# Keys and values of an attention block from float32r parts in three passes, and a sum of squares moved to GpSimd

## The chip, the cores and the metric

One core of a Trainium2 chip runs the whole program as a single launch. The metric is device time in microseconds (us), the median of several executions. Below, PE is the matmul engine (TensorE) and PEld its weight loads, DVE is VectorE, ACT is ScalarE, POOL is GpSimd, and SP is the queue engine that issues most transfers.

## The reference

A block of a hybrid model over 512 tokens and 16 meta tokens (T = 528 rows), all in float32. What matters here is the latent attention: queries, keys and values of 16 heads come from two small normalised latents, `cq` (384 wide) and `ckv` (256 wide).

```python
n1 = _rmsnorm(h, norm1_g[l])
xr, gr, cq, ckv, kr, g_rnn, g_att = jnp.split(n1 @ w_in[l], IN_SPLITS, axis=-1)
hr = _rg_lru(_causal_conv(xr, ...), ...)
y_rnn = (hr * jax.nn.gelu(gr)) @ w_rnn_out[l]
q = (_rmsnorm(cq, q_norm_g[l]) @ w_uq[l]).reshape(B, Tp, 16, 64 + 32)
kv = (_rmsnorm(ckv, kv_norm_g[l]) @ w_ukv[l]).reshape(B, Tp, 16, 64 + 64)
o = _mla_attention(q_nope, q_rope, kv[..., :64], k_rope, kv[..., 64:])
y_att = o @ w_attn_out[l]
mixed = jax.nn.sigmoid(g_rnn) * y_rnn + jax.nn.sigmoid(g_att) * y_att
h = h + mixed @ w_out[l]
h = h + _peer(_rmsnorm(h, norm2_g[l]), ...)    # 8 heads choose 16 of 16384 experts per token
```

## The kernel before

Everything is laid out with features on the 128 partitions. Most products are taken in three passes of float32r matmuls (`mm3`): each operand is split into a high part, cast by ACT, and a low part, subtracted by DVE (`split`), and high x high, high x low and low x high are added in PSUM. A few small products are plain float32 matmuls; the profile shows each of these as two records.

The stages follow one another:

- From 0 to about 48 us: norms, and the latents. `sq` holds their squares; `bcast_rms` multiplies them by a matrix of ones (float32) to sum over partitions and spread the sum, once for each 128-wide part: two parts for `ckv` (`kvn`), three for `cq` (`qn`).
- To about 184 us: the recurrent branch (`xr_tile`, `gates`, `gr_tile`, `gate_att`). `latent_norms` (line 300) is traced inside its first step, after `xr_tile(1)`: reciprocals of the two norms (`rk`, `rq`), and the latent `kvf` scaled to its final value.
- To about 472 us: attention, interleaved with the output of the recurrent branch (`out_rnn`) and the last `gate_att` tiles, which serve as work for PE between the steps of the attention. The heads go in eight pairs. `att_pair(pr)` makes the keys and values of a pair and asks for the query weights `wa`; it is called in the middle of the pair before, `att_query` later in it.
- Then the mixing, the choice of experts, and from about 960 us the dense and gathered expert products, to the end.

The order on each engine is made at compile time by a list scheduler: of the instructions that are ready it takes the one written first. Three shared resources matter in the attention:

- `wload` streams weights through a ring: three raw tiles (`RB`) and three split tiles (`WB`) of 512 columns (five in the stage before). `wa` takes two of the three split tiles from its cast to the last query product, `wgn` and `wrnn` of `out_rnn` two each. The weights of keys and values have a private tile, `wkv`, in plain float32, outside the ring.
- All products that `att_pair` and `att_query` make go through one PSUM tile, tag `am` (`rings`, line 446): the next product starts when ACT and DVE have taken the last one out.
- `vms`, `vfh`, `vfl` hold the values of two pairs in turn.

Of the kernel before, what the change touches and what calls it, by code (L numbers as in the profile page):

```python
# [8 lines left out]
F32 = mybir.dt.float32  # L9
F32R = mybir.dt.float32r  # L10
# [9 lines left out]
P = 128  # L20
D = 1024
NK = 8
NM = 16
S = 512
# [40 lines left out]
def r32(t):  # L65
    return t.bitcast(F32)
# [52 lines left out]
def hybrid_block_kernel(ctx: ExitStack, tc, hT, x, win, wkr, vecs, wgate, wrnn, watt, wuq, wukv, wout,  # L119
# [4 lines left out]
    def pool(stack, name, side="left", **kw):  # L124
        return stack.enter_context(tc.tile_pool(name=name, bufs=1, side=side, reuse_waits="tile", **kw))
# [21 lines left out]
    onesP = cp.tile([P, P], F32, name="onesP")  # L147
    one_t = cp.tile([P, 1], F32, name="one_t")
    eps_t = cp.tile([P, 1], F32, name="eps_t")
    efx = [cp.tile([P, NS], F32, name=f"efx{c}") for c in range(4)]  # L150
    gate = [cp.tile([P, NS], F32, name=f"gate{c}") for c in range(4)]
    ky = cp.tile([P, 2, P], F32, name="ky")

    def split(dst_hi, dst_lo, src):
        A.copy(dst_hi, src)  # L155
        V.tensor_sub(dst_lo, src, r32(dst_hi))  # L156
# [28 lines left out]

    cqh = fa.tile([P, 3, S], F32R, name="cqh")
    cql = fa.tile([P, 3, S], F32R, name="cql")
    kvf = fa.tile([P, 2, T], F32, name="kvf")
    tabq = fa.tile([P, S], F32, name="tabq")

    kth = [fa.tile([P, T], F32R, name=f"kth{i}") for i in range(NKB)]
# [11 lines left out]
    def bcast_rms(sq, pieces, dim, dst, name):  # L203

        for t0, n in pieces:
            o = mm1(f"{name}_ss{t0}")
            for k, q in enumerate(sq):
                TE.matmul(o[:, :n], onesP, q[:, t0:t0 + n], start=k == 0, stop=k == len(sq) - 1)
            A.activation(dst[:, t0:t0 + n], o[:, :n], AF.Sqrt, bias=eps_t, scale=1.0 / dim)
# [58 lines left out]
    krt = rg_tile("gr", "krt")  # L268
    tk, ka, kr = krt[0:64, 0, :], krt[64:96, 1, :], krt[64:96, 2, :]
    mk = rp.tile([P, P], F32, name="mk")  # L270
    nc.sync.dma_start(tk, cst[0:64, 768:768 + T])
    nc.sync.dma_start(ident, cst[:, 0:128])
    nc.sync.dma_start(mk, cst[:, 128:256])
    nc.sync.dma_start(tabq, cst[:, 256:768])
    nc.sync.dma_start(iota, cst[:, 1312:1440])
    nc.sync.dma_start(cand_f, cst[:, 1888:1888 + NCAND])
    nc.sync.dma_start(ky, keysT.rearrange("p (a n) -> p a n", a=2))
    V.tensor_mul(tk, tk, rb[0:64, :])
    sq = two(("rr", "ii"), "sq2")
    for k in range(2):  # L280
        for t0, n, o in lat[k]:
            V.tensor_mul(kvf[:, k, t0:t0 + n], o[:, :n], rb[:, t0:t0 + n])
        A.activation(sq[k], kvf[:, k, :], AF.Square)
    for k in range(3):
        (t0, n, o), = now(proj_tile(k, False, f"wcq{k}"))
        cq = hp.tile([P, S], F32, tag="sg", bufs=2, name=f"cq{k}")
        gk = vec[:, V_QG + k:V_QG + k + 1]
        V.tensor_mul(cq, o, rb[:, NM:])
        A.activation(sq[2 + k][:, :S], cq, AF.Square)
        A.activation(cqh[:, k, :], cq, AF.Identity, scale=gk)  # L290
        V.scalar_tensor_tensor(cql[:, k, :], cq, gk, r32(cqh)[:, k, :], op0=OP.mult, op1=OP.subtract)
    for t0, n, o in now(proj_tile(None, True, "wkr", wkr, 64)):
# [1 line left out]
        V.tensor_mul(kr[:, t0:t0 + n], o[32:64, :n], tk[32:64, t0:t0 + n])  # L294
    rk = rp.tile([P, T], F32, name="rk")
    rq = rp.tile([P, S], F32, name="rq")
    bcast_rms(sq[0:2], TT, 256, rk, "kvn")
    bcast_rms(sq[2:5], ((0, S),), 384, rq, "qn")

    def latent_norms():  # L300

        V.tensor_add(kr, kr, ka)
        split(kth[0][64:96, :], ktl[0][64:96, :], kr)
        for i in range(NKB):
            for r0 in (64, 96):
                if (i, r0) != (0, 64):
                    nc.gpsimd.dma_start(kth[i][r0:r0 + 32, :], kth[0][64:96, :])
                    nc.gpsimd.dma_start(ktl[i][r0:r0 + 32, :], ktl[0][64:96, :])
        V.reciprocal(rk, rk)
        for k in range(2):  # L310
            V.scalar_tensor_tensor(kvf[:, k, :], kvf[:, k, :], vec[:, V_KVG + k:V_KVG + k + 1], rk,
                                   op0=OP.mult, op1=OP.mult)
        V.reciprocal(rq, rq)
        V.tensor_mul(tabq, tabq, rq)
        V.tensor_copy(ident_b, ident)
        V.tensor_copy(mask_b, mk)
# [139 lines left out]
    def mma(name):  # L456
        return ps_ring("att", name)
# [9 lines left out]


    MK = 64 + NM
    vms = [ap.tile([P, P], F32R, name=f"vm{i}") for i in range(2)]  # L470
    pms = [ap.tile([P, 2 * P], F32R, name="pm")]
    zero = ap.tile([P, T], F32, tag="p", bufs=PB, name="zero")
    V.memset(zero, 0.0)
    for t in vms + pms:
        V.tensor_copy(t, zero[:, :t.shape[-1]])

    def att_pair(pr):

        wkv = ap.tile([P, 2, 2, P], F32, tag="wkv", bufs=1, name=f"wkv{pr}")
        nc.sync.dma_start(wkv, wukv[pr].rearrange("p (a k m) -> p a k m", a=2, k=2))  # L480
        vh = ap.tile([P, 4, P], F32R, tag="vfh", bufs=2, name=f"vfh{pr}")
        vl = ap.tile([P, 4, P], F32R, tag="vfl", bufs=2, name=f"vfl{pr}")
        vm = vms[pr % 2]
        for t0, n in TT:
            o = mma(f"k{pr}_{t0}")
            for k in range(2):
                TE.matmul(o[:, :n], wkv[:, 0, k, :], kvf[:, k, t0:t0 + n], start=k == 0, stop=k == 1)
            if t0:
                for k in range(2):
                    TE.matmul(o[:NM, 384:512], kvf[:, k, 0:NM], wkv[:, 1, k, :], start=k == 0, stop=k == 1)  # L490
                A.copy(vm[0:NM, :], o[:NM, 384:512])
                A.copy(vm[32:32 + NM, :], o[:NM, 384:512])
                V.tensor_sub(vm[64:64 + NM, :], o[:NM, 384:512], r32(vm)[0:NM, :])
            for j in range(2):
                b = (2 * pr + j) % NKB
                A.copy(kth[b][0:64, t0:t0 + n], o[64 * j:64 * j + 64, :n])
                V.tensor_sub(ktl[b][0:64, t0:t0 + n], o[64 * j:64 * j + 64, :n], r32(kth[b])[0:64, t0:t0 + n])

        o = mma(f"v{pr}")
        for c in range(4):  # L500
            t0 = NM + c * P
            for k in range(2):
                TE.matmul(o[:, c * P:(c + 1) * P], kvf[:, k, t0:t0 + P], wkv[:, 1, k, :], start=k == 0, stop=k == 1)
        split(vh, vl, o.rearrange("p (c m) -> p c m", m=P))
        pair = dict(v=(vh, vl, vm), w=wload(wuq[pr], 768, f"wa{pr}"), q=[])
        return pair

    def att_query(pr, j, pair):

# [205 lines left out]
    ctx.enter_context(dx)  # L715
    actp = pool(dx, "act", "right")
    vp = pool(dx, "vstream", "right")
    po_ = pool(postx, "choice")
    scx = ExitStack()
    sp_ = pool(scx, "scat", "right")  # L720
    tv = [po_.tile([P, PH, 2, TOPK], F32, name=f"tv{i}") for i in range(4)]
# [317 lines left out]
def _layout(i):  # L1039
    f = {k: np.asarray(v) for k, v in i.items()}  # L1040
    x = f["x"].reshape(S, D)
    h = np.concatenate([f["meta_tokens"], x], 0)
    a = {}
    a["hT"] = h.T.reshape(NK, P, T).transpose(1, 0, 2).reshape(P, NK * T)
    a["x"] = x

    def tiles(w):
        kk, n = w.shape
        return w.reshape(kk // P, P, n // P, P).transpose(2, 1, 0, 3).reshape(n // P, P, kk)

    w = f["w_in"][0]
    o = np.cumsum([0, 1024, 1024, 384, 256, 32, 1024, 1024])
    xr, gr, cq, ckv, kr, grn, gat = (w[:, o[j]:o[j + 1]] for j in range(7))
    a["win"] = np.concatenate([tiles(t) for t in (cq, ckv, xr, gr, grn, gat)], 0)
    krs = np.concatenate([kr, kr[:, 16:32], kr[:, 0:16]], 1)
    a["wkr"] = krs.reshape(NK, P, 64).transpose(1, 0, 2).reshape(P, NK * 64)
    col = lambda v: v.reshape(-1, P).T
    a["vecs"] = np.concatenate([col(f["norm1_g"][0]), col(f["conv_w"][0].reshape(-1)), col(f["conv_b"][0]),
                                col(f["rg_ba"][0]), col(f["rg_bx"][0]), col(f["rg_lambda"][0]), col(f["q_norm_g"][0]),
                                col(f["kv_norm_g"][0])], 1)  # L1060
    a["wgate"] = np.stack([f["rg_wa"][0], f["rg_wx"][0]], 0).transpose(1, 2, 0, 3).reshape(NK, P, 2 * P)
    a["wrnn"] = tiles(f["w_rnn_out"][0])
    a["watt"] = tiles(f["w_attn_out"][0])
    uq = f["w_uq"][0].reshape(3, P, NH, 96)
    uq = np.concatenate([uq, uq[..., 80:96], uq[..., 64:80]], -1)
    uq = uq.reshape(3, P, 8, 2, P).transpose(2, 1, 3, 0, 4).reshape(8, P, 768)
    kv = f["w_ukv"][0].reshape(2, P, 8, 2, 2, 64)
    kv = kv.transpose(2, 1, 4, 0, 3, 5).reshape(8, P, 512)
    a["wuq"], a["wukv"] = uq, kv
    a["wout"] = f["w_out"][0].reshape(NK, P, 2, 512).transpose(2, 0, 1, 3)  # L1070
    a["wq"] = tiles(f["peer_wq"][0])
    a["keysT"] = np.concatenate([f["peer_keys1"][0].T, f["peer_keys2"][0].T], 1)
    a["g2"] = f["norm2_g"][0]
    a["gf"] = f["final_g"]
    a["peer_u"] = f["peer_u"][0]
    a["peer_uT"] = f["peer_u"][0].reshape(NJ, P, NK, P).transpose(0, 3, 2, 1).reshape(NJ, P, D)
    a["peer_v"] = f["peer_v"][0]
    a["cst"] = _consts()
    return {k: np.ascontiguousarray(v) for k, v in a.items()}
# [16 lines left out]
```

## Time and profile before

| | |
|---|---|
| median of 3 runs | 1863.19 us (1859.29 to 1865.14) |
| the profiled execution: time | 1864.08 us |
| its span, first to last instruction | 1862.3 us |
| mean granted TensorE clock | 0.994 of 2.4 GHz |
| PE busy | 1811.8 us, 97% of the span |
| PEld, DVE, ACT, POOL busy | 86%, 78%, 52%, 19% |

A row of the timeline gives the start, the duration, engine, line, operation and operands; `x4` means four instructions merged. PE rows overlap: a matmul's end is modelled, so the price of one is read from the distance between starts, not from its duration.

### The profile page before, as it was taken

Reading aid. Unit: us, or ns where it says so; the run is one execution under the profiler, and the core shown is the slowest. Engines: PE = TensorE matmul, PEld = TensorE weight load, DVE = VectorE, ACT = ScalarE, POOL = GpSimd, SP = SyncE. Lnnn points to the kernel's source line nnn. Section 1 sums busy time; section 2 is a strip of 40 time slices with the busy share of each in tenths; the row PEclk is TensorE's granted clock in tenths of the full one; section 3 lists DMA queues with packets and bytes.
Section 4 is the critical chain, followed back from the end, with each engine's and each line's share of the span. In section 5 each row is a group of like instructions: output and inputs, shape, how many; then the busy total and the mean of one; then the engine's idle time right before and its main releaser. Section 6 shows DMA issues by size and latency. Waiting matters only on the chain.

```text
span 1862.3 us, 28323 instructions
## 1 busy us (share of the span) xinstructions
PE 1811.8 (97%) x9731; PEld 1601.3 (86%) x9731; DVE 1444.0 (78%) x3088; ACT 968.5 (52%) x2011; POOL 355.2 (19%) x295
## 2 busy tenths in 40 slices
PE   8999999999899999999999999999999999999997
PEld 7888778877778889998999999999999999997886
DVE  7787677777546999997558788877888878887775
ACT  6778576766333337999953333433333333333343
POOL 0100000000100000000014344434444443543310
PEclk9999999999999999999999999999999999999999
DMA  5333212112743223445589999998998989988764
GB/s 163 96 98 105 74 55 66 57 60 75 237 131 125 80 85 125 177 164 193 191 295 336 324 322 352 318 315 307 321 332 310 322 310 322 333 300 272 266 219 153
DMA packets 181600, 390.32 MB, mean 210 GB/s; under 512 B 16593, under 2 KB 68305, under 8 KB 179921
## 3 DMA queue, kind: packets, MB, share of 16 engines
q1 hardware_dynamic: 141632, 245.97, 39.0%
q0 software_dynamic: 39536, 142.00, 22.1%
q8 instruction: 76, 1.25, 0.3%
q10 hardware_dynamic: 288, 0.56, 0.1%
q14 instruction: 68, 0.55, 0.1%
HBM read 353.44 MB, written 34.08 MB: 208 GB/s over the span
## 4 chain that ended last, share of the span: by engine, by line
PE 30%; issue 16%; POOL 6%; DMA 5%; DVE 4%; ACT 1%; DVEq 0%; POOLq 0%; ACTq 0%
PE y L183 5%; PE y L181 5%; PE y L182 5%; PE a L183 4%; POOL v L915 4%; PE a L181 4%; PE a L182 4%; PE sc L869 4%; DMA v<-in_peer_v_dram,eidx 3%; POOL u L915 2%; DMA u<-in_peer_u_dram,eidx 1%; DVE hot L884 1%; DMA gt<-gd 1%; DMA ut_w<-in_peer_uT_dram 0%; DVE ut_l L156 0%
## 5 line engine op out<-in xcount | busy, mean ns | idle before, releaser
L183 PE MATMUL a<-xdh,ut_l 128*128 128x384 f32 x1024 | 347.4, 339 | 9.2 <-DVE ut_l L156 9.2
L181 PE MATMUL a<-xdh,ut_h 128*128 128x384 f32 x1024 | 348.6, 340 | 1.7 <-ACT ut_h L155 1.4
L182 PE MATMUL a<-xdl,ut_h 128*128 128x384 f32 x1024 | 345.5, 337 | 0.3 <-DVE xdl L156 0.3
L155 ACT CAST ut_h<-ut_w 128x512 fp32r<-128x512 f32 x256 | 157.8, 624 | 327.2 <-DMA ut_w<-in_peer_uT_dram 277.9
L181 PE MATMUL y<-vh,ch 128*128 128x512 f32 x768 | 299.6, 390 | 5.4 <-ACT ch L155 5.4
L183 PE MATMUL y<-vh,cl 128*128 128x512 f32 x768 | 301.6, 393 | 0.0
L182 PE MATMUL y<-vl,ch 128*128 128x512 f32 x768 | 301.0, 392 | 0.0
L915 POOL DMA_INDIRECT u<-in_peer_u_dram,eidx x128 | 161.4, 1261 | 666.3 <-DMA gt<-gd 441.4
L915 POOL DMA_INDIRECT v<-in_peer_v_dram,eidx x128 | 175.4, 1370 | 266.8 <-DVE acc L935 239.7
L156 DVE TENSOR_TENSOR ut_l<-ut_w,ut_h 128x512 fp32r<-128x512 f32 x256 | 169.5, 686 | 54.5 <-ACT ut_h L155 51.3
L183 PEld LDWEIGHTS a<-xdh,ut_l 128*128 128x128 f32 x1024 | 194.1, 190 | 11.4 <-DVE ut_l L156 11.0
L181 PEld LDWEIGHTS a<-xdh,ut_h 128*128 128x128 f32 x1024 | 194.3, 190 | 6.1 <-ACT ut_h L155 2.3
L182 PEld LDWEIGHTS a<-xdl,ut_h 128*128 128x128 f32 x1024 | 194.1, 190 | 3.9 <-DVE xdl L156 0.5
L156 DVE TENSOR_TENSOR vl<-vr,vh 128x1024 fp32r<-128x1024 f32 x128 | 157.6, 1232 | 42.9 <-ACT vh L155 41.9
L155 ACT CAST ch<-gt 128x384 fp32r<-128x384 f32 x128 | 65.7, 513 | 232.4 <-DVE gt L965 227.7
L181 PEld LDWEIGHTS y<-vh,ch 128*128 128x128 f32 x768 | 144.7, 188 | 34.8 <-ACT ch L155 6.5
L935 DVE SCALAR_TENSOR_TENSOR acc<-v,coef,acc 128x1024 f32<-128x1024 f32 x128 | 164.1, 1282 | 10.5 <-DMA v<-in_peer_v_dram,eidx 8.5
L183 PEld LDWEIGHTS y<-vh,cl 128*128 128x128 f32 x768 | 144.4, 188 | 31.1 <-DVE cl L156 0.8
L182 PEld LDWEIGHTS y<-vl,ch 128*128 128x128 f32 x768 | 144.5, 188 | 28.5
L926 DVE SCALAR_TENSOR_TENSOR jk<-u,xn 128x1024 bf16<-128x1024 f32 x128 | 156.6, 1223 | 13.7 <-DMA u<-in_peer_u_dram,eidx 11.3
L155 ACT CAST vh<-vr 128x1024 fp32r<-128x1024 f32 x128 | 133.8, 1045 | 32.5 <-PE y L183 28.5
L156 DVE TENSOR_TENSOR cl<-gt,ch 128x384 fp32r<-128x384 f32 x128 | 71.5, 559 | 81.8 <-ACT ch L155 81.8
(348 smaller groups left out, 3470.2 us busy)
## 6 DMA issues: line engine op xcount, KB each, us to landing
ut_w<-in_peer_uT_dram SPq DMA_DIRECT2D x256, 256.0 KB, 6.1
vr<-in_peer_v_dram SPq DMA_DIRECT2D x128, 512.0 KB, 6.7
gd<-stg SPq DMA_DIRECT2D x12, 2048.0 KB, 7.3
gt<-gd SPq DMA_DIRECT2D x96, 256.0 KB, 6.8
wq_w<-in_wq_dram SPq DMA_DIRECT2D x32, 256.0 KB, 2.8
wxr_w<-in_win_dram SPq DMA_DIRECT2D x16, 256.0 KB, 2.8
wgr_w<-in_win_dram SPq DMA_DIRECT2D x16, 256.0 KB, 2.7
wga_w<-in_win_dram SPq DMA_DIRECT2D x16, 256.0 KB, 2.7
```

The costliest lines, as they stand in the source:

```text
L155: A.copy(dst_hi, src)
L156: V.tensor_sub(dst_lo, src, r32(dst_hi))
L181: TE.matmul(o, lh, rh, start=first, stop=False)
L182: TE.matmul(o, lh, rl, start=False, stop=False)
L183: TE.matmul(o, ll, rh, start=False, stop=last)
L869: TE.matmul(o[:, u * P:(u + 1) * P], hot[:, h + u, :], wj[:, h + u, :], start=True, stop=True)
L884: V.tensor_tensor(hot, iota.unsqueeze(1).to_broadcast([P, SG, P]), it[:, t0:t0 + SG].unsqueeze(2).to_broadcast([P, SG, P]), op=OP.is_equal)
L915: G.indirect_dma_start(out=t, out_offset=None, in_=src, in_offset=bass.IndirectOffsetOnAxis(ap=eidx[:, s:s + 1], axis=0))
L926: V.scalar_tensor_tensor(jk, t, 1.0, xn2, op0=OP.mult, op1=OP.mult, accum_out=coef[:, s:s + 1])
L935: V.scalar_tensor_tensor(acc, t, coef[:, s:s + 1], acc, op0=OP.mult, op1=OP.add)
```

## The change

Four things are edited. The scaled latent `kvf` is split into `kvh` and `kvl`, and the weights of keys and values come through `wload`, split as well; keys and values are then float32r products in three passes. Values are made for two pairs at once (`att_values`, called for even pairs), with a streamed operand of 256 columns; those of the 16 meta tokens become a product of their own. The squares of the latents are added on GpSimd before `bcast_rms`, which then has one part each. `efx`, `gate` and `ky` leave the constants for pools opened later; `ky` is loaded at the start of the choice of experts.

```diff
-    efx = [cp.tile(...)], gate = [cp.tile(...)], ky = cp.tile([P, 2, P], F32, name="ky")
...
-    kvf = fa.tile([P, 2, T], F32, name="kvf")
+    kvh = fa.tile([P, 2, T], F32R, name="kvh")
+    kvl = fa.tile([P, 2, T], F32R, name="kvl")
...
+    kvf = rp.tile([P, 2, T], F32, name="kvf")
...
-    nc.sync.dma_start(ky, keysT.rearrange("p (a n) -> p a n", a=2))
...
         A.activation(sq[k], kvf[:, k, :], AF.Square)
+    G.tensor_add(sq[0], sq[0], sq[1])
...
         A.activation(sq[2 + k][:, :S], cq, AF.Square)
+        if k:
+            G.tensor_add(sq[2][:, :S], sq[2][:, :S], sq[2 + k][:, :S])
...
-    bcast_rms(sq[0:2], TT, 256, rk, "kvn")
-    bcast_rms(sq[2:5], ((0, S),), 384, rq, "qn")
+    bcast_rms(sq[0:1], TT, 256, rk, "kvn")
+    bcast_rms(sq[2:3], ((0, S),), 384, rq, "qn")
...
+            split(kvh[:, k, :], kvl[:, k, :], kvf[:, k, :])       # in latent_norms, after kvf is scaled
...
-    vms = [... for i in range(2)]
+    vms = [... for i in range(3)]
...
+    def att_values(pr):
+        w = wload(wukv[pr // 2][:, 512:1024], 512, f"wv{pr}")
+        for i in range(2):
+            vals[pr + i] = (vfh tile, vfl tile, vms[(pr + i) % 3])         # bufs=3
+        for c2 in range(0, 4, 2):
+            o = mma(f"v{pr}_{c2}")
+            for c in range(2):
+                t = slice(NM + (c2 + c) * P, NM + (c2 + c + 1) * P)
+                for k in range(2):
+                    mm3(o[:, c * 256:(c + 1) * 256], kvh[:, k, t], kvl[:, k, t], *wsl(w, k, 256), k == 0, k == 1)
+            for i in range(2):
+                vh, vl, vm = vals[pr + i]
+                split(vh[:, c2:c2 + 2, :], vl[:, c2:c2 + 2, :], o.rearrange("p (c i m) -> p c i m", c=2, i=2)[:, :, i, :])
+        o = mma(f"vm{pr}")
+        for k in range(2):
+            mm3(o[:NM, :256], kvh[:, k, 0:NM], kvl[:, k, 0:NM], *wsl(w, k, 256), k == 0, k == 1)
+        for i in range(2):                     # for each pair two copies on ACT, one subtraction on DVE
...
     def att_pair(pr):
-        wkv = ap.tile([P, 2, 2, P], F32, tag="wkv", bufs=1, name=f"wkv{pr}")
-        nc.sync.dma_start(wkv, ...)
+        w = wload(wukv[pr // 2][:, pr % 2 * 256:pr % 2 * 256 + 256], 256, f"wk{pr}")
         for t0, n in TT:
             o = mma(f"k{pr}_{t0}")
             for k in range(2):
-                TE.matmul(o[:, :n], wkv[:, 0, k, :], kvf[:, k, t0:t0 + n], start=k == 0, stop=k == 1)
-            if t0: ...                         # values of the meta tokens: 2 matmuls, 3 copies
+                mm3(o[:, :n], *wsl(w, k), kvh[:, k, t0:t0 + n], kvl[:, k, t0:t0 + n], k == 0, k == 1)
             ...                                # kth and ktl as before
-        o = mma(f"v{pr}")
-        ...                                    # 8 matmuls of 128 columns, one split of 512
+        if pr % 2 == 0:
+            att_values(pr)
+        return dict(v=vals.pop(pr), w=wload(wuq[pr], 768, f"wa{pr}"), q=[])
...
+    kp = pool(dx, "chosen", "right")           # efx and gate
     po_ = pool(postx, "choice")
+    ky = po_.tile([P, 2, P], F32, name="ky")
+    nc.sync.dma_start(ky, keysT.rearrange("p (a n) -> p a n", a=2))
```

## Rows read from the trace of the kernel before

**Rows 1.** Busy time per engine by stretch: attention, and the expert products.

```profile
250.00:300.00 50.00, 49.52 (x297) 40.64 (x296) 39.37 (x114) 33.28 (x88) 0.00 (x0) 1.00 0.19 59
...
1000.00:1200.00 200.00, 200.00 (x1013) 182.16 (x1012) 165.66 (x260) 75.14 (x124) 85.13 (x68) 1.00 0.94 328
```

**Rows 2.** Timeline of PE around the sums of squares.

```profile
44.07 1.94 PE L208 MATMUL kvn_ss<-sq_rr,onesP 128*128 128x264 f32 x8
45.85 1.88 PE L208 MATMUL qn_ss<-sq_rr,onesP 128*128 128x512 f32 x4
...
48.67 0.40 PE L228 MATMUL wxr_ps<-n1l,wxr_h 128*128 128x264 f32 x2
...
57.70 0.41 PE L228 MATMUL wxr_ps<-n1h,wxr_l 128*128 128x264 f32 x2
```

**Rows 3.** Timeline of DVE after the sums, and PE's first gate product.

```profile
52.71 3.35 DVE L313 RECIPROCAL rq<-rq 128x512 f32<-128x512 f32 x1
56.09 0.77 DVE L375 TENSOR_TENSOR xp<-wxr_ps,rb 128x264 f32<-128x264 f32 x2
...
62.00 0.76 PE L181 MATMUL g<-cvh,gw_h 128*128 128x264 f32 x4 [1.69 <-ACT cvh L155]
```

**Rows 4.** Timeline of PE at the start of the attention (first pair).

```profile
184.23 1.05 PE L487 MATMUL k<-kvf,wkv 128*128 128x264 f32 x4
184.92 0.58 PE L228 MATMUL wgn_ps<-n1h,wgn_h 128*128 128x512 f32 x1
...
192.89 1.95 PE L503 MATMUL v<-wkv,kvf 128*128 128x128 f32 x16
...
195.38 0.39 PE L228 MATMUL wgn_ps<-n1h,wgn_l 128*128 128x512 f32 x1
196.24 0.50 PE L181 MATMUL q<-cqh,wa_h 128*128 128x512 f32 x1 [0.47 <-DVE vfl L156]
```

**Rows 5.** Timeline of PE: values of meta tokens, then output products.

```profile
245.79 0.61 PE L490 MATMUL k<-wkv,kvf 128*16 128x128 f32 x4
...
246.55 0.28 PE L182 MATMUL o<-pfl,vfh 128*128 128x256 f32 x1
...
247.73 0.28 PE L183 MATMUL o<-pfh,vfl 128*128 128x256 f32 x1
```

**Rows 6.** Timeline of PE: the fourth pair's keys, values, first query.

```profile
272.65 1.11 PE L487 MATMUL k<-kvf,wkv 128*128 128x264 f32 x4
...
282.66 2.02 PE L503 MATMUL v<-wkv,kvf 128*128 128x128 f32 x16
...
286.56 0.39 PE L181 MATMUL q<-cqh,wa_h 128*128 128x512 f32 x1
```

**Rows 7.** Timeline of ACT in the same stretch: casts of streamed weights.

```profile
266.54 0.62 ACT L155 CAST wa_h<-wa_w 128x512 fp32r<-128x512 f32 x1
272.36 0.41 ACT L155 CAST wa_h<-wa_w 128x256 fp32r<-128x256 f32 x1
...
277.64 0.62 ACT L155 CAST wgn_h<-wgn_w 128x512 fp32r<-128x512 f32 x1 [0.37 <-PE yr L182]
...
290.76 0.62 ACT L155 CAST wgn_h<-wgn_w 128x512 fp32r<-128x512 f32 x1 [0.28 <-ACT oth L155]
```

**Rows 8.** Groups by line and shape: a 256-column split taken from PSUM.

```profile
L156 DVE TENSOR_TENSOR pfl<-pt,pfh 128x256 fp32r<-128x256 f32 x16 | 6.7, 419 | 1.1 <-ACT pfh L155 0.6
L155 ACT CAST pfh<-pt 128x256 fp32r<-128x256 f32 x16 | 5.9, 372 | 4.2 <-PE pt L558 3.8
```

**Rows 9.** Instructions on the tile ky: minimum, median and maximum ns, first and last start.

```profile
L745 PE MATMUL sc<-ky,q x128: 270/275/377, 587.4 to 678.3; 128*128 128x128 f32 x128
L277 SPq DMA_DIRECT2D ky<-in_keysT_dram x1: 328/328/328, 11.9 to 11.9; - x1
```

**Rows 10.** Last square of a latent (ACT timeline); additions of squares on DVE.

```profile
39.44 0.63 ACT L289 ACTIVATE sq_ii<-cq 128x512 f32<-128x512 f32 x1
...
L265 DVE TENSOR_TENSOR sq_cv<-sq_cv,sq_aa x4: 700/701/709, 15.2 to 17.7; 128x528 f32<-128x528 f32 x4
```

More of the change, by code (lines that the diff above doesn't have):

```diff
@@ L149, in hybrid_block_kernel @@
     eps_t = cp.tile([P, 1], F32, name="eps_t")
-    efx = [cp.tile([P, NS], F32, name=f"efx{c}") for c in range(4)]
-    gate = [cp.tile([P, NS], F32, name=f"gate{c}") for c in range(4)]
-    ky = cp.tile([P, 2, P], F32, name="ky")
     def split(dst_hi, dst_lo, src):
@@ L469, in hybrid_block_kernel @@
     MK = 64 + NM
-    vms = [ap.tile([P, P], F32R, name=f"vm{i}") for i in range(2)]
+    vms = [ap.tile([P, P], F32R, name=f"vm{i}") for i in range(3)]
     pms = [ap.tile([P, 2 * P], F32R, name="pm")]
@@ L475, in hybrid_block_kernel @@
         V.tensor_copy(t, zero[:, :t.shape[-1]])
-    def att_pair(pr):
-        wkv = ap.tile([P, 2, 2, P], F32, tag="wkv", bufs=1, name=f"wkv{pr}")
[L480 to L483, printed above, removed]
+    vals = {}
+    def att_values(pr):
+        w = wload(wukv[pr // 2][:, 512:1024], 512, f"wv{pr}")
+        for i in range(2):
+            vals[pr + i] = (ap.tile([P, 4, P], F32R, tag="vfh", bufs=3, name=f"vfh{pr + i}"),
+                            ap.tile([P, 4, P], F32R, tag="vfl", bufs=3, name=f"vfl{pr + i}"), vms[(pr + i) % 3])
+        for c2 in range(0, 4, 2):
[11 more added lines that the diff above has]
+        for i in range(2):
+            vm, oi = vals[pr + i][2], o[:NM, i * P:(i + 1) * P]
+            A.copy(vm[0:NM, :], oi)
+            A.copy(vm[32:32 + NM, :], oi)
+            V.tensor_sub(vm[64:64 + NM, :], oi, r32(vm)[0:NM, :])
+    def att_pair(pr):
+        w = wload(wukv[pr // 2][:, pr % 2 * 256:pr % 2 * 256 + 256], 256, f"wk{pr}")
         for t0, n in TT:
@@ L486, in att_pair @@
             for k in range(2):
-                TE.matmul(o[:, :n], wkv[:, 0, k, :], kvf[:, k, t0:t0 + n], start=k == 0, stop=k == 1)
[L488 to L493, printed above, removed]
+                mm3(o[:, :n], *wsl(w, k), kvh[:, k, t0:t0 + n], kvl[:, k, t0:t0 + n], k == 0, k == 1)
             for j in range(2):
@@ L497, in att_pair @@
                 V.tensor_sub(ktl[b][0:64, t0:t0 + n], o[64 * j:64 * j + 64, :n], r32(kth[b])[0:64, t0:t0 + n])
-        o = mma(f"v{pr}")
[L500 to L506, printed above, removed]
+        if pr % 2 == 0:
+            att_values(pr)
+        return dict(v=vals.pop(pr), w=wload(wuq[pr], 768, f"wa{pr}"), q=[])
     def att_query(pr, j, pair):
@@ L717, in hybrid_block_kernel @@
     vp = pool(dx, "vstream", "right")
+    kp = pool(dx, "chosen", "right")
+    efx = [kp.tile([P, NS], F32, name=f"efx{c}") for c in range(4)]
+    gate = [kp.tile([P, NS], F32, name=f"gate{c}") for c in range(4)]
     po_ = pool(postx, "choice")
+    ky = po_.tile([P, 2, P], F32, name="ky")
+    nc.sync.dma_start(ky, keysT.rearrange("p (a n) -> p a n", a=2))
     scx = ExitStack()
```

4 lines of the change are left out of this document (3 added, 1 removed).

## The prediction

> **What bounds the kernel now.** I read the busy time by stretch first [rows 1]. In 50 us of attention PE is busy for 49.52, DVE for 39.4 and ACT for 33.3; in 200 us of the expert products PE is busy throughout. So PE sets the pace on both sides, and time that the attention gains or loses moves everything behind it: nothing there is tied to a clock time, and the gathers, which run beside PE at the end, start later or earlier with it. A busy PE is not yet a PE at its peak, so I then read the timeline for the distance between starts. Eight float32 records of 264 columns take 1.78 us from the first of kvn to the first of qn, 0.2225 each [rows 2]. Float32r records of 264 columns run at 0.122: 37 steps of two from 48.67 to 57.70 [rows 2]. With 256 columns it is 0.118: ten steps from 246.55 to 247.73 [rows 5]. A 512-column record I price at 0.236, by columns from the 264.
>
> **What the edits save on PE.**
> Sums of squares: kvn goes from 8 records to 4, 0.89 less. The qn records end at 48.43 (the row at 48.67 follows two wxr records of 0.122), so six take 2.58 and two will take 0.86. Together 2.6 us.
> Keys: a product of 264 columns is now two k of two records, 0.89, and becomes six of 0.122, 0.73. Sixteen of them: 2.6 us.
> Values: a pair's 16 records run from 192.89 to three 512-column records before 195.38, that is to 194.67 [rows 4]: 1.78. Two pairs, 3.56, become 24 records of 0.118, 2.83. Four times 0.73: 2.9 us.
> Values of the meta tokens: four records, between 0.45 (4 x 0.112, the pace of the 16 above) and 0.64 (245.79 to one step before 246.55 [rows 5]). I take 0.54; eight make 4.3, against 4 x 6 x 0.118 = 2.8: 1.5 us.
> In the attention this makes 7.0 us, 9.6 with the sums.
>
> **What of it reaches the end: the sums.** After the sums PE runs two wxr tiles and then waits 1.69 us for cvh at 62.00 [rows 3]. That wait comes from DVE: the reciprocal of rq runs from 52.71 for 3.35 us, and only then come xp at 56.09 and the chain from it to cvh. The change puts two more subtractions of 528 columns into this queue, right before rq, each about 0.70 by an addition of the same shape [rows 10]. If the order stays, xp comes 1.4 later, PE's 2.6 us turn into waiting and 1.4 are lost. But the products that xp waits for end 2.6 us earlier; if the scheduler then sees xp ready before it starts rq, the reciprocal goes behind, and 2.6 + 1.7 = 4.3 are gained. Bounds: +1.4 and -4.3. The deciding moments lie within a microsecond of each other, so I take the middle, -1.4.
>
> **The additions on GpSimd.** The last square is done at 40.07 [rows 10] and its sum is wanted behind kvn, at about 44.96, so 4.9 us of wkr and kvn products hide one addition; only what exceeds that would stop PE, one for one. No row has an elementwise operation on POOL; DVE's takes 0.70. The next things in POOL's queue are copies of kth, which wait for the rotated keys anyway. I take nothing. The Trainium skill (GPSIMD Engine Reference, 3.1 Elementwise) measures such an addition at 1.96 times VectorE's time; the estimate from it, 1.4 us, leaves the sum as it is, and no run here shows it yet.
>
> **The chain at the start of the attention.** All of att_pair's products pass through one PSUM tile, so each waits until ACT and DVE have emptied it. The first pair goes from 184.23 to its first query product at 196.24, 12.0 us [rows 4]. PE's own part is 0.89 + 0.89 + 0.54 + 1.78 = 4.1; 24 wgn records fill 5.7 (the first and the last are in the rows); 2.2 are empty. After v the tile takes 196.24 - 194.67 = 1.6 to empty; the other two hand-overs, with PE's filler in them, take 6.3. The change gives the first pair the values of two pairs, in two products, and a third for the meta tokens. Own part: 2 x 0.73 + 2.83 + 0.71 = 5.0. A value product now leaves in two splits of 256 columns, 2 x (0.372 + 0.419) = 1.6 [rows 8], one after the other, about 1.9 with its hand-over. The chain becomes 5.0 + 6.3 + 2 x 1.9 = 15.1.
> What fills its 10.1 us outside its own part? The ring has three split tiles. Before, wkv was outside it and wa held two, which left one for wgn. Now wk, wv and wa are all written ahead of wgn and want four. If they get them first, no wgn is there until the meta tokens are done, and 10.1 - 2.2 = 7.9 us are lost. If a wgn tile slips in as before, next to nothing is. That weights are cast in the order in which they are written is what rows show for wa [rows 7], so I stay nearer the upper end: +5.0.
>
> **The chain in the later even pairs.** In the fourth pair the chain from keys to query takes 13.9 us [rows 6]; the longer one, by 3.1, hits the third, fifth and seventh. There PE has the scores of the pair before to work on, so part is covered. Without cover: 3.1 less PE's added 0.9, and the one filler tile that is cast in this stretch (at 277.64; the next at 290.76 [rows 7]), 12 x 0.236 = 2.8, is displaced: 5.0 each. With it: nothing. As before PE shows next to no gap here, I take 1.2, three times: +3.6. The odd pairs have a chain shorter by v and its hand-over; with PE full that gains nothing beyond the records counted above.
>
> **Costed at nothing.** Splits of weights and values add some 7 us each to ACT and DVE over the whole attention, and both have a fifth and more of it free [rows 1]; where they sit in the chain they are counted there, and if that room were gone they would add to it one for one. ky is loaded later: one issue of 0.33 us [rows 9], with the wq weights queued behind it on SP, and wanted at 587.4; at worst 0.4. One more vm tile is cleared; efx, gate and kvf only change place.
>
> **Sum.** 1864.1 (profiled time) - 1.4 - 7.0 + 5.0 + 3.6 = 1864.3. The median of the runs is 0.9 below the profiled execution: 1863.4, so 1863. I forecast no change that can be measured (within 0.3%, 5.6 us). With every bound at its good end it is 1863.2 - 7.0 - 4.3 = 1852; at its bad end 1863.2 - 7.0 + 1.4 + 7.9 + 15.0 = 1881.
>
> **The rivals.**
> 1. Faster: the scheduler finds filler for the longer chains, and the sums' 2.6 us reach the end. -7.0 - 2.6 + 1.5 = -8.1: 1855. For it: PE shows hardly a gap in the attention, so the scheduler has managed with one filler tile so far. Against it: the tile that it managed with is the one now wanted.
> 2. Slower: the ring and the one PSUM tile starve PE. Start +7.9, three even pairs at 4.0, the sums -1.4: -7.0 + 18.5 = +11.5: 1875. It decides once the chains lose over 7.0 + 1.4 + 5.6 = 14 us. For it: wa already holds two of three tiles for some 20 us of a pair [rows 7]. Against it: while att_pair waits, the scores of the pair before can run. The Trainium skill (Perfetto Trace Analysis, Matmuls) says that independent groups of matmuls should rotate through several PSUM banks so that emptying one overlaps the next; the change adds groups to a single bank, and by that rule this rival's 1875 is the outcome. The trace agrees in part: the first chain shows the hand-overs, the later ones are covered.
> 3. Three passes save nothing over float32: the records at 0.122 and 0.118 against 0.2225 for half a product speak clearly against it; I give it no chance of its own.
>
> **Chances.** Forecast 0.36, first rival 0.33, second 0.31; they are those of within 0.3%, faster and slower. The range that leaves out no more than 2 in 10 runs from 1852 to 1876; the forecast's own is 1858 to 1869.
>
> **What would show it.** Records per product: six for keys, 24 for two pairs' values, kvn 4, qn 2. The sums: whether the gate product starts before 62.0, and whether rq's reciprocal stands before or behind xp. The start: the distance from the first key product to the first query product, and the first wgn record between them. The later pairs: that distance in the third pair against the fourth. The forecast fails if PE's idle time in the attention stays as it was (then it is faster) or grows by over 14 us.

## The result

The changed kernel takes 1882.59 us (median of 7 runs, 1874.78 to 1889.09) against 1865.14 us for the kernel before in the same comparison: a ratio of 1.0093, with a 95% interval of 1.0074 to 1.0112. It is slower by some 17.4 us, and the forecast of 1863 (1852 to 1876) lies below it. The profiled execution took 1887.19 us, with a span of 1885.4 us.

Where the time went is read from the starts of single groups of matmuls. The first key product comes 1.1 us earlier than before (183.1 against 184.2), the first query product 7.6 later (203.8 against 196.2 [rows 4]), the last output product of the attention 20.7 later (484.9 against 464.2), the first product of the last stage 16.4 later (977.5 against 961.1). So nearly all of it arises between 184 and 485 us. The products of the last stage, before and after, with their first and last start:

```profile
L181 PE MATMUL y<-vh,ch x768: 387/389/628, 961.1 to 1852.4; 128*128 128x512 f32 x192
L178 PE MATMUL y<-vh,ch x768: 387/389/628, 977.5 to 1876.2; 128*128 128x512 f32 x192
```

What the profiled execution lies behind beyond that came up in the last stage, which takes from 888.5 to 899.1 us, first to last product, in all the traces of this case, whatever the kernel. The stretch from the last output product to that stage takes 490.9 to 496.5 us in the eleven kernels that make keys and values in the new way, against 495.7 to 498.7 in the four that do not. That is where 4 of the 20.7 us are regained; the cause of that is open.

PE's busy time from the first key to the last output product, before and after (PE, PEld, DVE, ACT and POOL busy, granted clock, DMA share, GB/s):

```profile
184.23:464.50 280.27, 274.71 (x1599) 221.28 (x1598) 211.74 (x612) 186.57 (x500) 1.11 (x2) 1.00 0.21 65
183.11:485.20 302.09, 275.08 (x1594) 224.80 (x1593) 218.05 (x634) 197.64 (x525) 1.12 (x2) 0.97 0.20 62
```

PE stands idle for 27.0 us in this stretch, where it was 5.6: a growth of 21.4, over the 14 that the prediction names as a sign of failing.

The sums first. Timeline of PE after the change, around the sums and the first gate product (it answers [rows 2, 3]):

```profile
43.95 1.05 PE L207 MATMUL kvn_ss<-sq_rr,onesP 128*128 128x264 f32 x4
44.84 1.02 PE L207 MATMUL qn_ss<-sq_rr,onesP 128*128 128x512 f32 x2
...
61.24 0.76 PE L178 MATMUL g<-cvh,gw_h 128*128 128x264 f32 x4 [3.65 <-ACT cvh L152]
62.55 0.42 PE L179 MATMUL g<-cvl,gw_h 128*128 128x264 f32 x1
62.77 0.42 PE L180 MATMUL g<-cvh,gw_l 128*128 128x264 f32 x1
```

The records fell as counted, 4 and 2. But PE's wait ahead of the gates grew from 1.69 to 3.65 us, and behind it records of 264 columns stand 0.22 apart instead of 0.122, so the gates begin only 0.76 earlier and their own products take longer. DVE's timeline in between:

```profile
52.99 0.77 DVE L378 TENSOR_TENSOR xp<-wxr_ps,rb 128x264 f32<-128x264 f32 x2
...
54.29 3.35 DVE L316 RECIPROCAL rq<-rq 128x512 f32<-128x512 f32 x1
57.55 0.67 DVE L382 SCALAR_TENSOR_TENSOR cv<-xp,vec,cv 128x528 f32<-128x528 f32 x1
```

`xp` did go ahead of rq's reciprocal, 3.1 us earlier than in [rows 3]. Then the three products that make `cv` waited behind that reciprocal instead.

The start of the attention, PE again (it answers [rows 4]):

```profile
183.11 0.28 PE L178 MATMUL k<-kvh,wk_h 128*128 128x264 f32 x1
...
186.45 0.36 PE L178 MATMUL k<-kvh,wk_h 128*128 128x264 f32 x1 [2.46 <-DVE ktl L516]
...
189.68 0.55 PE L178 MATMUL v<-wv_h,kvh 128*128 128x256 f32 x1 [2.26 <-DVE ktl L516]
190.03 0.41 PE L179 MATMUL v<-wv_l,kvh 128*128 128x256 f32 x1
190.24 0.41 PE L180 MATMUL v<-wv_h,kvl 128*128 128x256 f32 x1
...
194.45 0.55 PE L178 MATMUL v<-wv_h,kvh 128*128 128x256 f32 x1 [1.87 <-DVE vfl L153]
...
199.22 0.37 PE L178 MATMUL vm<-wv_h,kvh 128*16 128x256 f32 x1 [1.87 <-DVE vfl L153]
...
201.92 0.80 PE L227 MATMUL wgn_ps<-n1h,wgn_h 128*128 128x512 f32 x1 [1.25 <-ACT wgn_h L152]
...
203.79 0.63 PE L178 MATMUL q<-cqh,wa_h 128*128 128x512 f32 x1
```

Five products, and a wait ahead of each but the first, since each needs the tile that the one before it has not left. No wgn record stands in these waits, and four stand ahead of the query, where the kernel before had 24 in the whole chain. And the value records are 0.21 apart, not 0.118. The windows show why (columns as above):

```profile
184.00:188.00 4.00, 0.96 (x6) 0.78 (x6) 1.68 (x4) 1.90 (x5) 0.00 (x0) 1.00 0.43 131
188.00:192.00 4.00, 2.32 (x11) 2.35 (x12) 1.06 (x3) 0.52 (x2) 0.00 (x0) 0.57 0.22 66
192.00:196.00 4.00, 2.13 (x10) 1.86 (x10) 0.85 (x2) 0.74 (x2) 0.00 (x0) 0.50 0.00 0
```

After a stretch in which PE worked 0.96 of 4 us the granted clock went to 0.50, the 1.2 GHz level, and it stood there until 205.

The later pairs. In the same 50 us as in [rows 1] PE is now busy for 46.03 where it was 49.52:

```profile
250.00:300.00 50.00, 46.03 (x278) 37.07 (x278) 38.43 (x116) 33.44 (x95) 0.00 (x0) 1.00 0.19 59
```

PE's waits from 208 to 485 us, after the first pair (us in total, times, longest):

```profile
PE o L592 <- ACT pm L583: 3.8, 5, 1.5
PE pt L571 <- DVE p L559: 3.0, 7, 0.7
PE o L578 <- DVE otl L153: 2.6, 4, 1.0
PE wgn_ps L227 <- ACT wgn_h L152: 1.7, 3, 1.3
PE v L178 <- DVE vfl L153: 1.4, 2, 0.7
```

The same view of the kernel before, for its whole attention, 184 to 464 us, has little:

```profile
PE pt L558 <- DVE p L546: 2.1, 7, 0.7
PE o L579 <- ACT pm L570: 0.7, 2, 0.5
```

The distance from the first key to the first query product, 13.9 us in the third pair of the kernel before (239.4 to 253.3), is 19.4 now (251.5 to 270.9). Against the kernel before, the first query product of the third, fifth and seventh pair falls back by 7.4, 7.7 and 12.4 us on the pair ahead of it, and the pair behind each regains 6.1 to 8.4.

### The profile page after: what moved, and what is told of

It reads as the page before. It is cut to its first block, busy times and chain, and to the rows that moved or that the text cites. A ratio compares the mean times of both kernels' runs of the same rounds, so it can differ in the third digit from the quotient of the medians.

```text
span 1885.4 us, 28352 instructions
## 1 busy us (share of the span) xinstructions
PE 1811.0 (96%) x9715; PEld 1603.4 (85%) x9715; DVE 1452.1 (77%) x3111; ACT 975.4 (52%) x2033; POOL 360.6 (19%) x298
## 4 chain that ended last, share of the span: by engine, by line
PE 44%; issue 19%; DMA 13%; DVE 11%; POOL 6%; ACT 6%; DVEq 0%; SPq 0%; POOLq 0%; ACTq 0%
DMA ut_w<-in_peer_uT_dram 5%; POOL u L933 5%; PE sc L887 3%; PE y L180 3%; PE y L178 3%; PE y L179 3%; DMA u<-in_peer_u_dram,eidx 3%; PE a L180 3%; PE a L179 3%; PE a L178 3%; PE q L178 2%; DMA v<-in_peer_v_dram,eidx 2%; PE q L179 2%; PE q L180 2%; PE wgn_ps L227 2%
## 5 line engine op out<-in xcount | busy, mean ns | idle before, releaser
L153 DVE TENSOR_TENSOR ut_l<-ut_w,ut_h 128x512 fp32r<-128x512 f32 x256 | 169.4, 686 | 60.8 <-ACT ut_h L152 60.6
```

## The experiments

The theory after this reading: the values of two pairs need more hand-overs of the one PSUM tile, and neither at the start nor later is there enough filler for them; the lower clock adds to it, and the sums gain nothing. The rivals: it is the ring of split tiles, whatever the PSUM; or the sums cost the time; or the clock is beside the point. Differences in time below are differences of ratios to the kernel before times 1864 us; by the two intervals each is uncertain by 4 to 7 us. What is finer comes from the traces, one execution each. There, `kvn`, the first product that the change touches, begins between 43.3 and 45.4 us; so moments ahead of the attention are best compared by their distance from it.

**1. The sums alone**, in the kernel before:

```diff
+    G.tensor_add(sq[0], sq[0], sq[1])
...
+            G.tensor_add(sq[2][:, :S], sq[2][:, :S], sq[2 + k][:, :S])
...
-    bcast_rms(sq[0:2], TT, 256, rk, "kvn")
-    bcast_rms(sq[2:5], ((0, S),), 384, rq, "qn")
+    bcast_rms(sq[0:1], TT, 256, rk, "kvn")
+    bcast_rms(sq[2:3], ((0, S),), 384, rq, "qn")
```

> The kernel before with one part of the change alone: the squares added on GpSimd and the sums of squares over one part (kvn 4 records, qn 2). Theory (the sums hide on PE but the gate products wait for DVE instead): the first gate product comes 0.5 to 1.5 us earlier than 62.0 with a wait of over 3 us ahead of it, and the whole is 0 to 2.6 us faster than before. Rival (the additions, or a lower clock after the longer wait, cost more than the sums save): it is 2 to 6 us slower, and the granted clock behind the wait falls below 1.

Measured: 1.0015 (0.9998 to 1.0032), no gain. The first gate product comes at 61.3 behind a wait of 3.76 us, 0.7 earlier; the first key product comes 0.5 later than before (184.7). Here rq's reciprocal still stands ahead of `xp` (52.21 and 55.59), the other order than in the changed kernel. The windows of this run:

```profile
60.00:64.00 4.00, 2.69 (x12) 2.69 (x13) 3.72 (x8) 2.74 (x5) 0.00 (x0) 0.50 0.57 163
64.00:68.00 4.00, 4.00 (x26) 4.00 (x25) 2.80 (x6) 3.66 (x7) 0.00 (x0) 0.68 0.23 62
```

In the kernel before, the granted clock is 1.00 in both. The wait and the lower clock behind it take back what the records save. The wait is the theory's, the fall of the clock the rival's; the time, 2.8 us slower (0.4 faster to 6.0 slower), takes in the theory's lower end of 0 and the rival's 2 us and more, and decides nothing between them.

**2. The first pair in other PSUM tiles**, in the changed kernel:

```diff
-    def mma(name):
+    def mma(name, pr=1):
+        if pr == 0:
+            return ps.tile([P, 512], F32, tag="s", bufs=3, name=name)
...
-            o = mma(f"v{pr}_{c2}")
+            o = mma(f"v{pr}_{c2}", pr)
```

(the same for `vm` and `k`)

> The changed kernel, with the first pair's key, value and meta products in tiles of the three-buffer PSUM ring instead of the single PSUM tile. Theory A (the single PSUM tile makes the first chain long: five hand-overs of some 2 us each with nothing between): the first query product comes 9 to 12 us after the first key product instead of 20.7, the granted clock stays at 1, and the whole is 8 to 14 us faster than the changed kernel. Theory B (the ring of three split tiles, which leaves no wgn tile as filler, is the cause whatever the PSUM): the chain stays above 16 us and the whole gains under 4 us.

Measured: 1.0022 (1.0002 to 1.0041), 13.2 us faster than the changed kernel; from the first key to the last output product the trace is 14.9 us shorter. PE's timeline:

```profile
182.52 0.28 PE L178 MATMUL k<-kvh,wk_h 128*128 128x264 f32 x1
...
185.87 0.35 PE L178 MATMUL v<-wv_h,kvh 128*128 128x256 f32 x1 [0.30 <-DVE ktl L518]
...
188.05 0.40 PE L178 MATMUL q<-cqh,wa_h 128*128 128x512 f32 x1
```

The chain is 5.5 us, shorter than expected, with the clock at 1 throughout. It is also PE's own part of the prediction, 5.0, with one gap of 0.5: the records cost what was counted. Theory A holds for the start. The later pairs are as they were (the same waits, `o` for `pm` 3.8 us, `pt` 2.9, `otl` 2.6).

**3. The ring**, in the changed kernel: wa is loaded in the first query, and the generator takes a step ahead of it.

```diff
-        return dict(v=vals.pop(pr), w=wload(wuq[pr], 768, f"wa{pr}"), q=[])
+        return dict(v=vals.pop(pr), w=None, q=[])
...
+        if pair["w"] is None:
+            pair["w"] = wload(wuq[pr], 768, f"wa{pr}")
...
         pairs = {0: att_pair(0)}
+        yield
```

> The changed kernel, with wa loaded and cast in the first query instead of at the end of the pair's keys and values, and one more step of the generator of wgn ahead of the first queries, so that wa no longer holds two of the three split tiles during the chain. Theory B (the ring starves PE of wgn records): wgn records appear between the first key and the first query product, PE's empty time there falls from 11 to under 6 us, even pairs after the first lose less too, and the whole is 6 to 14 us faster than the changed kernel. Theory A (the hand-overs of the single PSUM tile): no filler or little, chain still 18 us or more, and the whole is within 4 us of the changed kernel; a query that has to wait for its wa can make it slower.

Measured: 1.006 (1.0038 to 1.0081), 6.2 us faster than the changed kernel. PE's timeline:

```profile
183.34 0.46 PE L227 MATMUL wgn_ps<-n1h,wgn_h 128*128 128x512 f32 x1
...
197.00 0.28 PE L178 MATMUL vm<-wv_h,kvh 128*16 128x256 f32 x1 [1.88 <-DVE vfl L153]
...
201.14 0.63 PE L178 MATMUL q<-cqh,wa_h 128*128 128x512 f32 x1
```

Both theories hold in part. 24 wgn records stand in the first three hand-overs, and PE's empty time, worked out from starts and prices, falls from 11.3 to 5.6 us; the hand-overs stay (chain 18.5 us), and from 198 to 204 the granted clock is still 0.50. That the later even pairs would lose less too was a miss: from the second pair on the queries lie 4 to 8 us ahead of the changed kernel's, and the lead does not grow from pair to pair. The ring took the filler away; the single tile is what made filler needed.

**4. The clock**, in the changed kernel, first pair only:

```diff
+    def warm(pr, n, name):
+        if pr == 0:
+            d = ps.tile([P, 512], F32, tag="s", bufs=3, name=name)
+            for i in range(n):
+                TE.matmul(d, cqh[:, 0, 0:P], cqh[:, 0, :], start=True, stop=True)
...
+            warm(pr, 8, f"wmv{c2}")      # behind each value product
...
+        warm(pr, 5, "wmm")               # behind the meta product
...
+            warm(pr, 9, f"wmk{t0}")      # behind each key product
```

> The changed kernel, with 38 further matmuls of 512 columns in the first pair (nine behind each key product, eight behind each value product, five behind the meta product), whose results are thrown away; they fill PE's waits and compute nothing that is wanted. Theory C (a part of the loss is the granted clock, which stands at half from 189 to 205): the clock stays at 1, value records stand 0.118 apart instead of 0.213, the first chain falls from 20.7 to 17 to 19 us, and the whole is 2 to 6 us faster than the changed kernel. Rival (the hand-overs on ACT and DVE set the chain and the clock of PE is beside the point): chain 20 us or more, the whole the same or 1 to 3 us slower.

Measured: 1.0081 (1.005 to 1.0111), which its time alone does not tell from the changed kernel. The further matmuls are 39, by the edit and in the trace, one more than the expectation says. In the trace the chain is 17.1 us (182.6 to 199.7) against 20.7, the first query product comes 4.1 and the last output product 4.9 us earlier. One of its windows:

```profile
192.00:196.00 4.00, 4.00 (x25) 3.42 (x24) 1.14 (x3) 0.89 (x3) 0.00 (x0) 1.00 0.00 0
```

The clock stays at 1 where it was 0.50, and value records stand 0.118 apart. So it made some 3.6 us of the chain, and the hand-overs the rest. About 4 of the 4.9 us are gone again by the first product of the last stage (976.4 against 977.5): the stretch between took 496.5 us in this execution and 492.6 in that of the changed kernel, within the spread given above.

**5 and 6. The ring of PSUM tiles for all pairs**: in 5 the values of every even pair, in 6 the keys of all pairs too.

```diff
-            o = mma(f"v{pr}_{c2}", pr)
+            o = mma(f"v{pr}_{c2}", 0)
...
-            o = mma(f"k{pr}_{t0}", pr)     # experiment 6 only
+            o = mma(f"k{pr}_{t0}", 0)
```

> The second experiment's kernel, with the value and meta products of every even pair, not of the first alone, in tiles of the three-buffer PSUM ring. There each of the second, third and fourth even pair still put the first query product 7 to 13 us later against the kernel before, of which the next pair gave back 6 to 8. Theory A (the single PSUM tile is the cause there as well): the even pairs lose 3 us or less each, PE's empty stretches of 2 to 3 us around the value and meta products go, the last output product of the attention comes 3 to 6 us earlier than in the second experiment, and the whole is 0.2 to 0.5% faster than the kernel before. Rival (the ring is the scores' own, and in the later pairs they need its three tiles): score products wait instead, the attention ends no earlier or up to 5 us later.

> The same with the key products of every pair in the three-buffer ring too; only the query products stay in the single tile. Theory A: at least as fast as the fifth experiment, up to 3 us faster. Rival (scores need the ring): 2 to 8 us slower than the fifth experiment, with waits of the scores for their tiles.

Measured: 0.9964 (0.9946 to 0.9981) and 0.9943 (0.9924 to 0.9963). The fifth is 10.8 us faster than the second and 0.36% faster than the kernel before, as expected; its last output product comes 8.5 us earlier (460.9 against 469.4), more than expected. From the first key to the first query product the third pair takes 12.1 us (237.4 to 249.5), and no even pair's query falls back by more than 1.4 us on the pair ahead of it, against the kernel before. PE's busy time, first key to last output product:

```profile
183.86:461.20 277.34, 267.56 (x1594) 219.40 (x1593) 218.65 (x634) 195.85 (x524) 1.11 (x2) 1.00 0.21 67
```

It is 7.2 us below the kernel before; in the second experiment, with the same records, it is 5.1 below. Idle time is 9.8 us, in the second 17.6. PE's longest waits from 194 to 461 us in the fifth:

```profile
PE pt L573 <- DVE p L561: 2.1, 5, 0.7
PE o L580 <- DVE otl L153: 1.6, 3, 0.7
PE o L594 <- ACT pm L585: 1.3, 5, 0.4
```

The waits for `vfl` and for wgn_h are no longer in this view, and that of `o` for `pm` is down from 3.8 us: what stood behind the single tile were not the values alone. The rival fell: the scores wait 0.5 us in all, and a value product 0.2 for a tile of the scores. Keys in the ring gave another 3.9 us, with intervals that overlap; in the trace the stretch from the first key to the last output product is 2.8 us shorter (274.2 against 277.0).

**7. The fifth with the old sums** (experiment 1 undone in it).

> The fifth experiment's kernel, with the sums of squares as in the kernel before (no additions on GpSimd, kvn 8 records, qn 6). Theory (the sums' saving on PE only becomes a wait of 3.6 us ahead of the first gate product, behind which the granted clock falls): the wait there is 1 to 2 us, the clock stays at 1 from 60 to 68, the first key product comes within 0.7 us of that of the fifth experiment, and the whole is the same within 1 us. Rival (the saved records count): the first key product 1.5 to 2.6 us later and the whole as much slower.

Measured: 0.9965 (0.995 to 0.9981), the same as the fifth. The wait ahead of the gates is 1.73 us, the clock stays at 1 from 60 to 68, the first key product comes at 184.4, 0.5 behind the fifth, as forecast. From the start of `kvn` it comes 140.2 us later; with the new sums (the changed kernel and experiments 2 to 6) it comes 139.0 to 139.8 later. So of the 2.6 us saved by the sums 0.4 to 1.2 reach the attention, too little for the times to show.

**8. The control**: the edit of experiment 2 in the kernel before.

> The kernel before, with the first pair's key and value products in the three-buffer PSUM ring. Theory (a hand-over of the single tile costs only where no filler is at hand; in the kernel before 24 wgn records filled nearly all of the 7.9 us): the distance from the first key to the first query product falls from 12.0 to 4 to 6 us, the wgn records come later instead, and the whole is 0 to 2 us faster. Rival (the single tile by itself costs the chain, filler or not): 5 us or more faster.

Measured: 1.0001 (0.9988 to 1.0013). PE's timeline:

```profile
183.50 1.94 PE L489 MATMUL k<-kvf,wkv 128*128 128x264 f32 x8
...
187.72 0.48 PE L181 MATMUL q<-cqh,wa_h 128*128 128x512 f32 x1
```

The chain falls from 12.0 to 4.2 us and the time does not move, within some 2 us: its hand-overs were full of work that now comes later. In the trace the stretch from the first key to the last output product is 1.6 us shorter (278.4 against 280.0), about the 2.2 us that were empty before. So in this pair the single tile costs what stays empty, and no more. The same control for the later pairs was not run; that rotating their tiles would give nothing in the kernel before is not shown.

**9, 10 and 11. rq's reciprocal written later**, behind the first gates: in the changed kernel (9), in the sixth (10), in the kernel before (11).

```diff
+    def query_norm():
         V.reciprocal(rq, rq)
         V.tensor_mul(tabq, tabq, rq)
...
             gates(j, *cs)
+            if hb == 0 and j == 0:
+                query_norm()
```

> The changed kernel with one thing moved: the reciprocal of rq, its product with the query table and the two copies of constants behind them come after the first gate products, not ahead of the products that make cv. Theory (this DVE work, 3.35 + 0.69 us, keeps the saving of the sums from PE, and the granted clock falls behind the wait): PE's wait ahead of the first gate product falls from 3.65 to under 1 us, the clock stays at 1 from 60 to 68, the first key product comes 3 to 6 us earlier than in the changed kernel, and the whole is as much faster. Rival (something else is late there, or DVE is late for it afterwards): the first key product less than 1 us earlier.

> The sixth experiment's kernel (key, value and meta products in the three-buffer ring) with the same move. If the two causes are separate, their gains add: 3 to 6 us faster than the sixth experiment, some 0.7 to 0.9% faster than the kernel before. If the start of the attention is bound by something else, no faster than the sixth.

> The kernel before with the same move. Its wait ahead of the first gate product was 1.69 us and its clock did not fall, so the theory gives 1.5 to 2 us: first key product at 182.3 to 182.8 instead of 184.2. The first key product of the ninth experiment should then be 2 to 2.6 us ahead of this one, which is the sums' saving on PE once DVE lets it through; under 1 us would say that the sums save nothing even then.

Measured: 1.0096 (1.0073 to 1.0119), 0.9957 (0.9932 to 0.9983) and 1.0001 (0.9987 to 1.0015), in each the time of the kernel it was made from. All three expectations of a gain missed, for one reason, shown by DVE's timeline in the ninth:

```profile
54.31 0.77 DVE L384 SCALAR_TENSOR_TENSOR cv<-xp,vec,cv 128x528 f32<-128x528 f32 x1
55.00 3.34 DVE L318 RECIPROCAL rq<-rq 128x512 f32<-128x512 f32 x1
58.27 0.67 DVE L384 SCALAR_TENSOR_TENSOR cv<-xp,vec,cv 128x528 f32<-128x528 f32 x1
```

The reciprocal went to DVE between two products of `cv`, in the tenth too (56.83); in the eleventh it stayed ahead of `xp` (51.91). By the scheduler's rule that is where DVE had nothing else ready. The wait ahead of the gates stayed at 3.69 us in the ninth and tenth, and at 1.69 in the eleventh. These runs say nothing on the theory; a dependency is needed, not another line.

**12 and 13. The reciprocal held back**: the sixth with a true dependency (12), and the same with the old sums (13).

```diff
+    def query_norm(late):
+        V.scalar_tensor_tensor(rq[:, 0:1], late, 0.0, rq[:, 0:1], op0=OP.mult, op1=OP.add)
         V.reciprocal(rq, rq)
...
+                query_norm(rr[:, 0, 0:1])
```

> The sixth experiment's kernel, with rq's reciprocal made to depend on a first result of the gates (one column of rq gets zero times a gate value added), since moving its line did not move it in DVE's queue. Theory (the reciprocal ahead of cv's products keeps the sums' saving from PE): DVE goes from xp straight to cv's products, PE's wait ahead of the first gate product falls from 3.65 to under 1 us, the granted clock stays at 1 from 60 to 68, the first gate product comes 2.5 to 4 us earlier (60.8 before that) and the first key product 3 to 6 us earlier than in the sixth experiment; the whole 0.15 to 0.3% faster than the sixth. Rival (another chain, of cvh or of the gate weights, is as late): first gate product less than 1 us earlier.

> The twelfth experiment's kernel with the old sums (kvn 8 records, qn 6, no additions on GpSimd). If the shorter sums save on PE what their records say, its first key product comes 2 to 2.6 us behind that of the twelfth experiment; if they save nothing even with DVE cleared, less than 0.7 us behind.

Measured: 0.993 (0.9909 to 0.9952) and 0.9957 (0.9936 to 0.9977). PE in the sixth, then DVE and PE in the twelfth, then PE in the thirteenth:

```profile
43.49 1.05 PE L207 MATMUL kvn_ss<-sq_rr,onesP 128*128 128x264 f32 x4
...
60.78 1.04 PE L178 MATMUL g<-cvh,gw_h 128*128 128x264 f32 x4 [3.65 <-ACT cvh L152]
```

```profile
54.78 0.77 DVE L385 SCALAR_TENSOR_TENSOR cv<-xp,vec,cv 128x528 f32<-128x528 f32 x1
...
57.35 0.76 DVE L385 SCALAR_TENSOR_TENSOR cv<-xp,vec,cv 128x528 f32<-128x528 f32 x1
```

```profile
44.07 1.05 PE L207 MATMUL kvn_ss<-sq_rr,onesP 128*128 128x264 f32 x4
...
58.83 0.76 PE L178 MATMUL g<-cvh,gw_h 128*128 128x264 f32 x4 [1.12 <-DVE xp L381]
```

```profile
44.85 1.94 PE L207 MATMUL kvn_ss<-sq_rr,onesP 128*128 128x264 f32 x8
...
60.95 0.28 PE L178 MATMUL g<-cvh,gw_h 128*128 128x264 f32 x1
```

The wait fell to 1.12 us (a little above the 1 expected) and the clock stayed at 1. The first gate and the first key product come 2.0 us earlier than in the sixth (58.8 against 60.8, 180.6 against 182.6). But this execution reached `kvn` 0.6 us later; from there the gate product comes 2.5 us earlier (14.8 against 17.3), as expected, and the key product 2.6 (136.5 against 139.1), a little less than the 3 expected. The time lies 2.4 us below the sixth's, with intervals that overlap, so the gain is shown by the trace alone.

In the thirteenth the first gate product comes without a wait, 2.1 us later than in the twelfth; from `kvn` it is 1.3 later (16.1 against 14.8). The first key product comes 5.4 later (4.7 from `kvn`), not 2 to 2.6, since there the second gate product waits 2.15 us (at 70.8) and the granted clock falls behind it (0.72 from 70 to 76). So with DVE cleared the shorter sums bring the gates forward by about 1.3 us: the 2.6 saved, less the wait that is left. The twelfth has the lowest ratio here; it is faster than both kernels, and not told from the sixth.

## Why the prediction was wrong

- **PE's records: right.** Six records for a key product at 0.122, 24 of 0.118 for the values of two pairs, 4 and 2 for the sums. The second experiment shows the first pair's own part as it was counted, with its hand-overs gone, and PE's busy time in the attention falls by 5.1 us in the second and 7.2 in the fifth, where 7.0 were counted.
- **The sums: -1.4 taken, -0.4 to -1.2 found at the first key product (experiment 7), nothing that a time shows.** Of the two cases weighed, the one priced at -4.3 came: `xp` went ahead of rq's reciprocal. What was not followed is the rest of the chain to `cvh`: the products of `cv` come behind the same reciprocal. That the number taken lies near is luck, the middle of two cases of which neither came as reasoned. In the kernel before the sums alone made the key product 0.7 us later from `kvn` (experiment 1); 12 and 13 show half of the saving arrive at the gates once DVE is free.
- **The additions on GpSimd: right at nothing.** The last took 1.28 us, where the prediction's estimate was 1.4, and ended at 43.23, before qn, which wants it, began at 44.84:

```profile
41.95 1.28 POOL L291 TENSOR_TENSOR sq_rr<-sq_rr,sq_ii 128x512 f32<-128x512 f32 x1 [5.52 <-ACT sq_ii L289]
```

- **The chain at the start: +5.0 taken and +7.9 as its worst end, 12.6 found.** This is the step that failed first. Its mechanism was right, the sizes were not. The four hand-overs put at 10.1 us (6.3 and two of 1.9) measured 9.4: from the start of the last record before it plus its price to the next start, as 183.72 + 0.12 to 186.45, they are 2.6, 2.4, 2.2 and 2.2. A fifth, of the meta product, was not in the sum: 1.9 empty around the first wgn record, and 0.9 for four such records ahead of the query. The rest, 3.5, is put down to the lower clock, and the fourth experiment, which keeps it at 1, takes off 3.6: 15.1 - 0.7 + 2.8 + 3.5 = 20.7. So 9.4 + 1.9 empty and 3.5 of clock, 14.8, less the 2.2 that were empty before, make 12.6; the second experiment gives 13.2 back (14.9 in the trace). The bound of 7.9 knew neither the fifth hand-over nor the granted clock, and of its two cases the bad one came, no filler until the meta tokens are done, where 5.0 of the 7.9 were taken.
- **The later even pairs: +3.6 taken, +15.0 as the worst end, about 10.8 found** by the fifth experiment against the second. The reasoning was that PE shows next to no gap there before. That says that the old chain was covered, not that a longer one would be; this step was wrong in its reasoning and not only in size. And the term asked only about the chain itself: the view of waits shows the loss at `o` for `pm`, at `pt` and `otl` too, the pair before's own steps. How much of the 10.8 the change lost, and how much rotating would have gained anyway, is open without a control in these pairs.
- **The sum again**, with the measured terms: -7.0 + 12.6 + 10.8 and nothing for the sums makes +16.4, against 17.4 measured (3.5 either way). It is a weak check: 10.8 is itself a difference of the times that the sum is to explain. The idle time, which does not come from those times, points the same way: 21.4 us more after the change, and 4.2 more in the fifth experiment.
- **The rivals.** The first, that the scheduler finds filler, did not come; the +1.5 in its sum has no row behind it. The second, the ring and the one PSUM tile starving PE, is what happened, from the point it named (14 us lost in the chains; 23.4 were); its 1875 was too low for the same reasons. The rule that stood beside it, that independent groups of matmuls rotate through several PSUM banks (the Trainium skill, Perfetto Trace Analysis, Matmuls), is borne out by experiments 2 and 5, 13.2 and 10.8 us. The eighth bounds it: in the first pair of the kernel before, where nearly every hand-over had other work beside it, rotating gave nothing that the time shows.
- **Costed at nothing**: the later load of `ky` did nothing visible; its product starts 17.5 us later, as everything does there. The splits added 9.3 us to ACT and 6.9 to DVE in the attention (the fifth experiment against the kernel before), where some 7 each were taken.

## What to carry to other kernels

Saved matmul time counts only if the engine has something to do with it: before counting records, list what each product waits for and which filler is ready at that moment, and if the change takes the filler's buffers, price the chain without any. A place without gaps says that today's chain is covered, not how much more it would bear; when products are made longer or joined, let them rotate through several PSUM tiles. And where a saving ends in a wait, follow the waiting chain to its last operation, past the first one that moves.

## What the runs showed of the hardware

- The granted clock has a price of its own after waits. After the 3.76 us ahead of the gates it was 0.50 from 60 to 64 in the first experiment; after 1.69 us in the kernel before and 1.12 in the twelfth it stayed at 1.00. The length of a wait alone does not say whether a fall follows: ahead of an `ya` product near 500 us, 2.70 us in the kernel before left it at 1.00, and 2.42 us in the second experiment was followed by windows at 0.80 and 0.77.
- An addition on GpSimd of 128 x 512 elements took 1.28 and 1.30 us, one of 128 x 528 1.65, where DVE's of 528 took 0.70 [rows 10].
